# A hybrid layer on one core: the output projection's first half moved from behind the conv units to in front of them

## The chip, the cores and the metric

The kernel runs on one core of a Trainium2 chip. The metric is the device time of one execution in microseconds (us), as the median of several runs. The engines are TensorE (PE, the matmuls), VectorE (DVE), ScalarE (ACT), GpSimd (POOL) and SyncE (SP, which issues most DMAs). Each of them works through its own queue of instructions in order.

## What is computed

One layer over 576 frames (512 of a prompt, 64 of a running stream), 2048 wide, in float32:

```python
hn = rmsnorm(x, g_norm1)
q, k, v, gb, gc, hc = split(hn @ w_in)              # 3 x 1024 columns of heads, 3 x 1024 of conv
o_attn = stick_breaking_blocks(rmsnorm(q), rmsnorm(k), v)
u = gc * hc
o_conv = gb * causal_conv3(u)                       # 8 groups of 128 channels
mix = concat(rmsnorm(o_attn, g_attn_out), rmsnorm(o_conv, g_conv_out))
x = x + mix @ w_out                                 # first half of the rows: heads, second half: conv
h2 = rmsnorm(x, g_norm2)
x = x + (silu(h2 @ w_gate) * (h2 @ w_up)) @ w_down
```

Outputs are the new x, the new keys and values, and the last two rows of u. What matters here is `mix @ w_out`: its first half of the sum (over the 1024 head channels) needs only the attention, and its second half needs all conv groups.

## The kernel before

**Numbers in two parts.** Every float32 operand of a matmul is a pair of a rounded value and the rest (`split`, L222: a cast on ACT, a subtraction on DVE or POOL). A product of two operands takes three matmuls: high by high, low by high, high by low. Frames are cut in halves of 288 columns (`HALVES`).

**Seven products.** Where a weight block and the frames are each cut in 2 x 2 blocks, Winograd's form of Strassen's method does the work of eight block products in seven, with sums of blocks on either side. For the conv columns the sums of frames (`xs_dram`, made in `x_sums`, L581) are written to DRAM during the heads and loaded again (`load_sum`, L858, and L1111). For the first half of the output projection the sums of the normed head outputs are called forms; `head_forms` (L528) makes 28 blocks of them (7 forms, 4 blocks deep) from `o_half`, the two tiles that hold the attention's result.

**The stages.** (1) Heads: 24 column blocks of `w_in` by plain products, attention of one head beside the projection of the next. (2) Two conv groups by plain products (`conv_group`, L903, `STD` = 2, six column blocks). Beside them `head_forms` runs, spread over PE's work by a small planner: `Pipeline` (L66) counts a tick for each step of three matmuls, and a generator says with `yield n` after how many ticks its next instructions are placed. Each form is split into a staging tile and written to `form_dram`, 28 writes on SP (L553). (3) Nine conv units by seven products (`CU`, L934), six groups in pairs of u, u, b. (4) Eight output units by seven products over the forms, which are loaded back from `form_dram` in seven DMAs (`load_forms`, L1068). (5) The second half of the projection by plain products (`out_proj`, L1151) over the mix tiles of the conv groups, loaded from `mix_dram`. (6) The feed-forward part.

**Units and their order.** `conv_run(n, p)` does product p of unit n: 24 matmuls in a conv unit, 12 in an output unit. `conv_prepare(n, p)` (L967) casts and splits the weights of a product, four products ahead of PE (L1130), into four rotating places (`whl`); at product 6 it makes three sums of weight blocks on DVE (L974 to L976, the tile `s1`). `corder` (L1114) is the order of products, written out by hand. The raw weights lie in three places: two of 1 MB in `raw_tile`, and `raw_c` in the memory of the first attention tile; an output unit takes one of the first two for all its weights. `call_columns` (L942) loads the next weights when a place comes free. `done` (L1018) takes a finished block: a conv block goes through the taps, and `put_mix` (L515) scales it, adds its squares to the norm's sum and writes it to `mix_dram` on POOL's queue; an output block is added to the residual x in `x2`. The tiles of `put_mix`, and others, rotate in a ring of two (tag `hl`).

**Order on the engines.** PE works in the order of the text. For DVE, ACT and POOL, the compiler's list scheduler decides the order by what it reckons to be ready; SP's order is that of the text only in stretches with `manual_schedule` (before: from the last conv unit on, L1128). DMA loads are issued by SP and wait there, in order, for their place.

**At the seams.** Before the output units, the last conv unit has its products in another order (L1117), so that the places of the frame sums come free in time for the forms (L1132 to L1138). `open_out` (L1072) then opens the tiles for the residual and the mix, and `load_rest` and `group_scale` (L567) bring x and the norm's scale beside the output units.

Of the kernel before, what the change touches and what calls it, by code (L numbers as in the profile page):

```python
# [16 lines left out]
P = 128  # L17
# [77 lines left out]
def tile_hybrid_stream_step(  # L95
# [35 lines left out]
    form_dram = tc.dram_tile([FORMS, NH // 2, 2, P, HALF], F32, name="form_dram")  # L131
# [383 lines left out]
    def put_mix(g, i, src, gcol, acc, first):  # L515

        turns["mx"] = turns.get("mx", 0) + 1
        if "mx" in bt and turns["mx"] % 3 == 0:
            t = bt["mx"]
        else:  # L520
            t = tmp.tile([P, 2, HALF], F32R, tag="hl", name="mx")
        nc.scalar.activation(out=t[:, 0], in_=src, func=AF.Copy, scale=gcol)
        add_squares(acc, src, first)
        nc.vector.scalar_tensor_tensor(out=t[:, 1], in0=src, scalar=gcol, in1=t[:, 0].bitcast(F32),
                                       op0=ALU.mult, op1=ALU.subtract)
        nc.gpsimd.dma_start(out=mix_dram[i, g].rearrange("f p t -> p f t"), in_=t.bitcast(F32))

    def head_forms():  # L528
# [3 lines left out]
        turn = [0]  # L532
# [6 lines left out]
        yield 8  # L539
        for k in range(NH // 2):  # L540
            pair = o_half[k // 2][:, 2 * (k % 2) : 2 * (k % 2) + 2, :]
            four = pair.rearrange("p k (i t) -> p (k i) t", i=2)
            b11, b12, b21, b22 = (four[:, q, :] for q in range(4))
            for r in range(2):
                nc.vector.scalar_tensor_tensor(out=pair[:, r], in0=pair[:, r], scalar=col("ga", 2 * k + r), in1=acc_a,
                                               op0=ALU.mult, op1=ALU.mult)
            yield 2

            def put(f, src, lo_eng):
                t = bt["stage"][:, turn[0] % NP]  # L550
                turn[0] += 1
                split(t[:, 0], t[:, 1], src, lo_eng)
                nc.sync.dma_start(out=form_dram[f - 1, k].rearrange("f p t -> p f t"), in_=t.bitcast(F32))  # L553

            for f, src in ((1, b11), (2, b21), (3, b22)):
                put(f, src, nc.vector)
                yield 2
            for f, out, a, b in ((5, b11, b12, b11), (7, b12, b12, b22), (6, b22, b22, b11), (4, b21, b21, b22)):
                nc.gpsimd.tensor_tensor(out=out, in0=a, in1=b, op=ALU.subtract)
                yield 1  # L560
                put(f, out, nc.gpsimd if f in (5, 6) else nc.vector)
                yield 2
            if k == 1:
                bt["raw"] = apool.tile([P, 2048], F32, tag="oa", name="raw_c")
        load_sum(3)

    def group_scale(acc, dst, rows_of):  # L567

        four = cpool.tile([P, 2, 2, HALF], F32R, tag="uc", name="sqg")
        for i, (a, b) in enumerate(HALVES):  # L570
            sh, sl = four[:, i, 0], four[:, i, 1]
            split(sh, sl, acc[:, a:b])
            yield rows_of
            ss = channel_sums(sh, sl, a, b, "ssg")
            ms, t = (tmp.tile([P, HALF], F32, tag=tag, name=tag + "g") for tag in ("r", "sq"))
            rsqrt_mean(dst[:, a:b], ss, 8 * P, HALF, ms, t)
            yield rows_of
# [269 lines left out]
    def open_b():  # L847
# [14 lines left out]
    def open_units():  # L862
        cx = apool.tile([P, 1024 + UW + 2 * HALF], F32, tag="ob", name="cx")
        bt["mx"] = cx[:, 1024 + UW :].rearrange("p (f t) -> p f t", t=HALF).bitcast(F32R)
        bt["s1"] = cx[:, :1024].rearrange("p (j c) -> p j c", c=P)
        bt["c"] = cx[:, 1024 : 1024 + UW - 2]
# [27 lines left out]
    def put_o(g, i, t):  # L894
# [6 lines left out]
        put_mix(g, i, t, col("gc", g), bt["acc"][:, a:b], g == 0)  # L901

    def conv_group(g):  # L903
# [22 lines left out]
        if g == STD - 1:  # L926
            call_columns([2])
# [838 lines left out]
```

## Time and profile before

| | us |
|---|---|
| median of 3 runs | 2409.63 |
| lowest, highest | 2407.19, 2409.69 |
| the profiled execution | 2407.78 |
| its span, first to last instruction | 2406.1 |
| conv units, about | 504 to 711 |
| output units, about | 711 to 811 |
| second half of the projection, about | 811 to 912 |

Rows of the trace are read so. A row of the timeline has the start, the length, the engine, the line of the kernel, the operation, the tile written, an arrow and the tile read, the shape and a count; in brackets the idle time before it and what ended it. PEld is the loading of weights, which goes beside the matmuls. SPq rows are DMA issues: their length is that of the issue, not of the transfer. The clock that PE was granted is 0.997 of full speed over the whole span.

### The profile page before, as it was taken

To read this page: it belongs to the slowest core of one execution; us is meant where nothing else is said; L and a number is where in the kernel's file an instruction comes from. 1 tells how busy PE (TensorE), PEld (TensorE's weight loads), DVE (VectorE), ACT (ScalarE), POOL (GpSimd) and SP (SyncE) were. 2 spreads that over 40 slices of the span, in tenths; PEclk is the share of its full clock that TensorE was granted. 3 is DMA by queue.
4 is the path that set the end of the run, shared out by engine and by line. 5 is a ranking of instruction groups with operands and counts; after the bars stand their busy time and mean duration, and the time that the engine had idled before them with its cause. 6 is when DMAs were issued, how large, how long until landed. Compare 5 with 4: busy or idle time off the path is not lost.

```text
span 2406.1 us, 44221 instructions
## 1 busy us (share of the span) xinstructions
PE 2375.1 (99%) x17825; PEld 2363.2 (98%) x17825; DVE 1911.9 (79%) x2862; ACT 1166.1 (48%) x2091; POOL 293.9 (12%) x400
## 2 busy tenths in 40 slices
PE   8999999999999999999999999999999999999999
PEld 8999999999999999999999999999999999999999
DVE  7767776688888868988888888888888777887875
ACT  6656655444444445444444444444444444444454
POOL 1111111231112220000000000000000001431211
PEclk9999999999999999999999999999999999999999
DMA  7354433584367433444444434534444945885642
GB/s 255 116 152 139 143 111 95 188 277 125 101 213 253 143 129 107 148 145 150 135 135 150 152 118 155 160 112 157 150 128 142 335 139 188 231 234 196 201 130 80
DMA packets 504086, 386.05 MB, mean 160 GB/s; under 512 B 11855, under 2 KB 493001, under 8 KB 503881
## 3 DMA queue, kind: packets, MB, share of 16 engines
q1 hardware_dynamic: 496712, 371.40, 48.3%
q0 software_dynamic: 6448, 11.51, 2.1%
q8 instruction: 139, 2.28, 0.4%
q14 instruction: 67, 0.54, 0.1%
q10 hardware_dynamic: 720, 0.33, 0.0%
HBM read 296.47 MB, written 86.72 MB: 159 GB/s over the span
## 4 chain that ended last, share of the span: by engine, by line
PE 84%; DVE 8%; DMA 4%; ACT 2%; issue 1%; POOL 0%; SPq 0%; ACTq 0%; DVEq 0%; POOLq 0%
PE psy L1516 33%; PE psw L1516 16%; PE pj L214 12%; PE psx L1516 8%; PE pjo L214 4%; DVE whl L224 3%; PE psy L1006 2%; PE pw L1359 2%; DMA raw_a<-in_w_in_dram 1%; PE psw L1006 1%; PE psx L1006 1%; DMA raw_c<-in_w_in_dram 1%; DMA forms<-form_dram 1%; PE z L683 1%; ACT whl L223 0%
## 5 line engine op out<-in xcount | busy, mean ns | idle before, releaser
L224 DVE TENSOR_TENSOR whl<-raw_a,whl 128x1024 fp32r<-128x1024 f32 (+4 forms) x372 | 391.6, 1053 | 76.0 <-ACT whl L223 74.8
L1516 PE MATMUL psy<-t,whl 128*128 128x288 f32 x2916 | 436.6, 295 | 0.0
L1516 PE MATMUL psy<-h_s,whl 128*128 128x288 f32 x2724 | 410.9, 295 | 1.8 <-ACT part L1526 1.8
L223 ACT CAST whl<-raw_a 128x1024 fp32r<-128x1024 f32 (+4 forms) x372 | 327.0, 881 | 159.2 <-issue 37.1
L1516 PEld LDWEIGHTS psy<-t,whl 128*128 128x128 f32 x2916 | 402.8, 188 | 0.2
L214 PE MATMUL pj<-x,whi 128*128 128x288 f32 x1856 | 398.8, 300 | 0.3 <-DVE x L357 0.3
L1516 PEld LDWEIGHTS psy<-h_s,whl 128*128 128x128 f32 x2724 | 377.4, 188 | 2.3 <-ACT part L1526 2.2
L1516 PE MATMUL psw<-t,whl 128*128 128x288 f32 x2592 | 376.8, 295 | 0.0
L1516 PEld LDWEIGHTS psw<-t,whl 128*128 128x128 f32 x2592 | 353.7, 188 | 0.2
L214 PEld LDWEIGHTS pj<-x,whi 128*128 128x128 f32 x1856 | 307.7, 190 | 1.0 <-DVE x L357 0.6
L214 PE MATMUL pj<-x,wlo 128*128 128x288 f32 x928 | 275.2, 297 | 0.1
L224 DVE TENSOR_TENSOR whl<-raw_b,whl 128x1024 fp32r<-128x1024 f32 (+5 forms) x186 | 194.1, 1044 | 69.3 <-ACT whl L223 68.2
L223 ACT CAST whl<-raw_b 128x1024 fp32r<-128x1024 f32 (+5 forms) x186 | 161.1, 868 | 162.8 <-issue 69.4
L1526 ACT COPY part<-psy 128x288 f32<-128x288 f32 x237 | 94.4, 399 | 270.5 <-PE psy L1516 270.3
L214 PEld LDWEIGHTS pj<-x,wlo 128*128 128x128 f32 x928 | 175.8, 189 | 0.7 <-DVE wlo L424 0.3
L1516 PE MATMUL psx<-h_s,whl 128*128 128x288 f32 x1122 | 164.5, 294 | 0.0
L1516 PEld LDWEIGHTS psx<-h_s,whl 128*128 128x128 f32 x1122 | 154.0, 188 | 0.0
L1279 POOL DMA_DIRECT2D hid_dram<-form x3 | 2.2, 725 | 975.9 <-DVE form L224 974.0
L223 ACT CAST whl<-s 128x1024 fp32r<-128x1024 f32 (+5 forms) x79 | 70.1, 888 | 99.2 <-PE psw L1516 97.7
L177 DVE TENSOR_TENSOR wlo<-raw_a,whi 128x1024 fp32r<-128x1024 f32 (+1 forms) x80 | 98.2, 1242 | 7.7 <-ACT whi L176 6.1
L214 PE MATMUL pjo<-mixc,whi 128*128 128x288 f32 x512 | 101.7, 294 | 0.0
L176 ACT CAST whi<-raw_a 128x1024 fp32r<-128x1024 f32 (+1 forms) x85 | 85.6, 1024 | 18.4 <-PE pjo L214 8.6
(449 smaller groups left out, 3988.2 us busy)
## 6 DMA issues: line engine op xcount, KB each, us to landing
hid_dram<-form SPq DMA_DIRECT2D x147, 288.0 KB, 2.3
raw_a<-in_w_in_dram SPq DMA_DIRECT2D x41, 1024.0 KB, 6.4
raw_a<-in_w_gate_dram SPq DMA_DIRECT2D x23, 1024.0 KB, 6.2
raw_a<-in_w_up_dram SPq DMA_DIRECT2D x23, 1024.0 KB, 5.5
raw_b<-in_w_gate_dram SPq DMA_DIRECT2D x21, 1024.0 KB, 6.7
raw_b<-in_w_up_dram SPq DMA_DIRECT2D x21, 1024.0 KB, 6.6
h_s<-hid_dram SPq DMA_DIRECT2D x10, 2016.0 KB, 8.0
raw_a<-in_w_out_dram SPq DMA_DIRECT2D x16, 1024.0 KB, 5.2
```

The lines of the kernel that those rows point to most:

```text
L176: nc.scalar.copy(out=hi[:, a:b], in_=raw[:, a:b])
L177: lo_eng.tensor_tensor(out=lo[:, a:b], in0=raw[:, a:b], in1=hi[:, a:b].bitcast(F32), op=ALU.subtract)
L214: mm(ps, w_[:, k, csl], x_, start=(k == 0 and n == 0), stop=(k == nk - 1 and n == 2))
L223: nc.scalar.copy(out=hi, in_=src)
L224: (lo_eng or nc.vector).tensor_tensor(out=lo, in0=src, in1=hi.bitcast(F32), op=ALU.subtract)
L683: mm(zb[i], a_[:, kk], b_[:, q0:TP], start=(n == 0), stop=False, skip_group_check=True)
L1006: mm(ps, whl[:, w_, j, :], x_, start=(start and j == 0 and q == 0), stop=(j == m - 1 and q == 2), skip_group_check=True)
L1279: q.dma_start(out=hid_dram[fp][2 * n - 2 : 2 * n].rearrange("f p t -> p f t"), in_=t.bitcast(F32))
L1359: mm(pss[j, i], w_[:, k, j * P : (j + 1) * P], x_, start=(kk == 0 and k == 0 and n == 0), stop=(kk == 1 and k == 7 and n == 2))
L1516: mm(ps, whl[:, w_, j, :], x_, start=(start and j == 0 and q == 0), stop=(j == len(xs_) - 1 and q == 2), skip_group_check=True)
L1526: nc.scalar.copy(out=t, in_=st["y"])
```

## The change

The output units now come before the conv units, directly behind the two plain conv groups.

- **Forms stay on chip.** `head_forms` splits forms 1, 2, 3, 5, 6, 7 straight into three tiles (`ft`), which take the places that the frame sums had, and form 4 into the first attention tile's memory once its blocks have been used (two of its blocks are first made in a tile of the `hl` ring). Forms 1 and 2 are made for all four depths first, then 3, 5, 7, 6, and 4 last. `form_dram` goes, with 28 writes and 7 reads.
- **Residual.** Each output unit adds to two rows of x, loaded into one of two places in the second attention tile's memory (`load_residual`), and is stored to `oh_dram` (`store_half`); all of it is loaded into `x2t` at the end.
- **Frame sums.** The three big loads of frame sums (`load_sum`) are issued in the last output unit, each when the forms in its place have been used.
- **Weights.** `raw_c` and the taps' and `s1`'s tile are opened behind the output units (`open_groups`); an output unit's `s1` comes from the `hl` ring.
- **Last conv unit.** Its products run as 1, 2, 6, 3, 5, 7, 4, with products 3, 7 and 4 in banks of their own; the last groups' mix goes straight to its tile, the rest of the mix is loaded in seven pieces from `open_out` on, and the norm's scale is worked out half by half (`group_scale(1)`, `group_scale(0)`), with its column sums nine ticks behind their split. `out_proj` takes the second half of the frames first.
- **SP** keeps the order of the text from the end of the plain conv groups to the end of the units.

```diff
-    form_dram = tc.dram_tile([FORMS, NH // 2, 2, P, HALF], F32, name="form_dram")
+    oh_dram = tc.dram_tile([KD, P, T], F32, name="oh_dram")
...
     def head_forms():
...
+        def put(f, k, src, lo_eng):
+            split(ft[f][:, k, 0], ft[f][:, k, 1], src, lo_eng)
+
+        for r in range(2):
+            for k in range(NH // 2):
+                pair = o_half[k // 2][:, 2 * (k % 2) : 2 * (k % 2) + 2, :]
                 nc.vector.scalar_tensor_tensor(out=pair[:, r], in0=pair[:, r], scalar=col("ga", 2 * k + r), in1=acc_a,
                                                op0=ALU.mult, op1=ALU.mult)
+                yield 1
+                put(1 + r, k, blocks[k][2 * r], nc.vector)
                 yield 2
+        for k, (b11, b12, b21, b22) in enumerate(blocks):
+            put(3, k, b22, nc.vector)
+            yield 1
+            for f, out, a, b in ((5, b11, b12, b11), (7, b12, b12, b22), (6, b22, b22, b11)):
                 nc.gpsimd.tensor_tensor(out=out, in0=a, in1=b, op=ALU.subtract)
                 yield 1
+                put(f, k, out, nc.gpsimd if f in (5, 6) else nc.vector)
                 yield 2
+        moved = tmp.tile([P, 2, HALF], F32, tag="hl", name="t4")
...
+        ft[4] = apool.tile([P, NH // 2, 2, HALF], F32R, tag="oa", name="form4")
...
+    def group_scale(i):
+
+        a, b = HALVES[i]
+        sh, sl = parts("sqg")
+        split(sh, sl, bt["acc"][:, a:b])
+        yield 9
+        ss = channel_sums(sh, sl, a, b, "ssg")
...
-        bt["stage"] = bpool.tile([P, NP, 2, HALF], F32R, tag="t3", name="hf")
-        for q in (1, 2):
-            load_sum(q)
+        for q, (f, e) in {1: (1, 2), 2: (6, 7), 3: (5, 3)}.items():
+            t = bpool.tile([P, NP, 2, HALF], F32R, tag=f"t{q}", name=f"forms{q}")
+            ft[f], ft[e] = t[:, : NH // 2], t[:, NH // 2 :]
...
     def open_units():
+        ob = apool.tile([P, 2304], F32, tag="ob", name="ob")
+        bt["x2"] = [ob[:, q * 2 * T : (q + 1) * 2 * T].rearrange("p (k t) -> p k t", k=2) for q in range(2)]
+        bt["ob"] = ob
+        bt["s1"] = ob[:, :1024].rearrange("p (j c) -> p j c", c=P)
+        bt["c"] = ob[:, 1024 : 1024 + UW - 2]
+
+    def open_groups():
+        bt["mx"] = bt["ob"][:, 1024 + UW : 1024 + UW + 2 * HALF].rearrange("p (f t) -> p f t", t=HALF).bitcast(F32R)
+        bt["raw"] = apool.tile([P, 2048], F32, tag="oa", name="raw_c")
+        call_columns([2])
...
-    CU = [x for g in range(STD, NG, 2) for x in (("u", g), ("u", g + 1), ("b", g))]
-    NCU = len(CU)
-    CU += [("o", d) for d in range(DC)]
+    CU = [("o", d) for d in range(DC)]
+    NO = len(CU)
+    CU += [x for g in range(STD, NG, 2) for x in (("u", g), ("u", g + 1), ("b", g))]
+    LAST = len(CU) - 1
...
+            if n < NO:
+                s1 = tmp.tile([P, 2, HALF], F32, tag="hl", name="s1").rearrange("p f t -> p (f t)")
+                s1 = st["s1"] = s1[:, : m * P].rearrange("p (j c) -> p j c", c=P)
+            else:
+                s1 = st["s1"] = bt["s1"]
...
+            if (n, p_) in ((LAST - 1, 4), (LAST, 3)):
+                load_weight()
+            elif n >= NO or (n, 4 - p_) not in cregion:
                 call_columns([q])
...
+    def load_residual(n):
+        nc.sync.dma_start(out=bt["x2"][n % 2], in_=xt_dram[2 * n : 2 * n + 2].rearrange("k p t -> p k t"))
+
+    def store_half(n):
+        nc.sync.dma_start(out=oh_dram[2 * n : 2 * n + 2].rearrange("k p t -> p k t"), in_=bt["x2"][n % 2])
...
+        for i in (1, 0):
+            end = NG - 1 - i
+            for k in range(0, end, 2):
+                e = min(k + 2, end)
+                nc.sync.dma_start(out=mc[:, i, k:e].bitcast(F32), in_=mix_dram[i, k:e].rearrange("k f p t -> p k f t"))
+        for j in range(NP):
+            nc.sync.dma_start(out=x2t[j], in_=oh_dram[2 * j : 2 * j + 2].rearrange("k p t -> p k t"))
...
+    sp_mode = ExitStack()
+    sp_mode.enter_context(tc.manual_schedule(engines={mybir.EngineType.SP}))
...
     open_units()
+    for n in range(2):
+        load_residual(n)
+    corder = [(0, p_) for p_ in (1, 2, 6, 7, 5)]
+    for n in range(1, LAST + 1):
+        corder += [(n, 1), (n - 1, 3), (n - 1, 4), (n, 2), (n, 6)]
+        corder += [(n, p_) for p_ in ((7, 5) if n < LAST else (3, 5, 7, 4))]
+    for p_ in (6, 7):
+        conv_prepare(0, p_)
     for k_, (n, p_) in enumerate(corder):
         conv_run(n, p_)
         if k_ + 4 < len(corder):
             conv_prepare(*corder[k_ + 4])
+        if p_ == 2 and 1 <= n <= NO:
+            store_half(n - 1)
+        if p_ == 7 and 1 <= n < NO - 1:
+            load_residual(n + 1)
+        if n == NO - 1 and p_ in (2, 7, 3):
+            load_sum({2: 1, 7: 2, 3: 3}[p_])
+        if (n, p_) == (NO - 1, 4):
+            open_groups()
...
-                for i, (a, b) in enumerate(HALVES):
+                for i, (a, b) in reversed(list(enumerate(HALVES))):
```

More of the change, by code (lines that the diff above doesn't have):

```diff
@@ L539, in head_forms @@
         yield 8
+        blocks = []
         for k in range(NH // 2):
@@ new lines, in head_forms @@
+        for k, (b11, b12, b21, b22) in enumerate(blocks):
+            if k < 2:
+                nc.gpsimd.tensor_tensor(out=moved[:, k], in0=b21, in1=b22, op=ALU.subtract)
+                blocks[k][2] = moved[:, k]
+            else:
+                nc.gpsimd.tensor_tensor(out=b21, in0=b21, in1=b22, op=ALU.subtract)
+            yield 1
+        ft[4] = apool.tile([P, NH // 2, 2, HALF], F32R, tag="oa", name="form4")
+        for k in range(NH // 2):
+            put(4, k, blocks[k][2], nc.vector)
+            yield 1
@@ L1049, in conv_run @@
             st["u2"] = kept("t")
+        elif n == LAST:
+            if p_ == 3:
+                st["c"] = misc("ps3")[:, :HALF]
+                conv_multiply(st["c"], n, 3, True)
+            elif p_ == 5:
+                conv_multiply(st["y"], n, 5, False)
+                open_out()
+                st["part"] = kept("acc")
+                done(0, 1, st["c"], st["part"])
+            elif p_ == 7:
+                w = ps_z.tile([P, 512], F32, tag=f"z{n % 2 + 1}", name="psw")[:, :HALF]
+                conv_multiply(w, n, 7, True)
+                done(1, 1, w, st["part"])
+                st["w"] = tmp.tile([P, HALF], F32, tag="ms", name="part", bufs=1)
+                nc.vector.tensor_tensor(out=st["w"], in0=w, in1=st["u2"], op=ALU.add)
+                pipe.spawn(group_scale(1))
+            else:
+                w = ps_z.tile([P, 512], F32, tag="z0", name="ps4")[:, :HALF]
+                conv_multiply(w, n, 4, True)
+                done(1, 0, w, st["w"])
+                rest = group_scale(0)
+                pipe.spawn(rest, next(rest))
         elif p_ == 7:
```

114 lines of the change are left out of this document (25 added, 89 removed).

## The prediction, on record before the run

> **What bounds the kernel now.** I read the page's engine totals first, then TensorE's waits between 440 and 960 us (where every step of the change lies), then the windows of that stretch.
>
> ```profile
> span 2406.1 us, 44221 instructions
> PE 2375.1 (99%) x17825; PEld 2363.2 (98%) x17825; DVE 1911.9 (79%) x2862; ACT 1166.1 (48%) x2091; POOL 293.9 (12%) x400
> ```
>
> TensorE (PE) is busy for 99% of the span. The change removes and adds no matmul (counts below), so it can only win the places where PE stands still, or make new ones. Where they are (us in total, times, longest):
>
> ```profile
> PE psy L1006 <- DMA forms<-form_dram: 6.1, 1, 6.1
> PE psy L1006 <- DVE whl L224: 4.0, 1, 4.0
> ```
>
> Two waits stand out. What follows each costs too (start, length, count, idle before):
>
> ```profile
> 701.61 3.17 PE psx L1006 x24
> 731.37 1.59 PE psw L1006 x12
> ...
> 514.44 4.78 PE L1006 MATMUL psy<-x,whl 128*128 128x288 f32 x23 [4.04 <-DVE whl L224]
> 723.99 7.38 PE L1006 MATMUL psy<-forms,whl 128*128 128x288 f32 x36 [6.10 <-DMA forms<-form_dram]
> ```
>
> A product takes 3.17 us with 24 matmuls and 1.59 us with 12, so 0.132 us a matmul. After the wait of 4.04 us 23 matmuls took 4.78 us instead of 3.04 (1.7 lost again); after 6.10 us 36 took 7.38 instead of 4.76 (2.6). The sum is best read from how many matmuls each 20 us window lacks (windows: us, PE busy and count, PEld, DVE, ACT, POOL, PE clock, DMA share, GB/s; the first row is a full one):
>
> ```profile
> 540.00:560.00 20.00, 20.00 (x153) 20.00 (x152) 17.97 (x23) 8.15 (x11) 1.23 (x7) 1.00 0.36 106
> ...
> 500.00:520.00 20.00, 15.96 (x110) 15.72 (x109) 19.19 (x22) 8.26 (x15) 9.17 (x13) 0.91 0.90 300
> 520.00:540.00 20.00, 19.51 (x148) 19.28 (x147) 12.70 (x16) 7.40 (x9) 0.87 (x1) 1.00 0.75 247
> ...
> 680.00:700.00 20.00, 19.83 (x148) 19.36 (x147) 16.42 (x22) 7.86 (x10) 0.85 (x2) 1.00 0.52 166
> 700.00:720.00 20.00, 17.89 (x133) 17.39 (x132) 18.27 (x34) 9.61 (x22) 6.21 (x8) 1.00 1.05 367
> 720.00:740.00 20.00, 16.01 (x103) 16.04 (x104) 10.98 (x17) 5.89 (x12) 4.01 (x5) 0.83 0.73 271
> ...
> 800.00:820.00 20.00, 19.21 (x146) 18.97 (x145) 16.85 (x27) 9.94 (x18) 4.08 (x4) 1.00 0.52 163
> ```
>
> They lack 43+5+5+20+50+7 = 130 matmuls of 0.131 us: **17.0 us**, all of it at the seams of the stage. That is the most the change can win. In the middle (540 to 680 us in conv units, 740 to 800 us in output units) nothing is lost.
>
> **The change, part by part.**
>
> *Unchanged:* 8 output units of 7 products with 12 matmuls (672) and 9 conv units of 7 with 24 (1512), only in the other order. DVE gains two additions of 288 columns in the last unit (0.46 us each by the L1029 row below).
>
> *Removed, 17.0 us.* The seam at 503.76 us goes: PE waited there for weights that landed late in the third place (`raw_c`). So does the seam at 710 to 731 us: 28 form writes and 7 form reads vanish, and no output unit follows a conv unit any more. With it goes the turned-round last conv unit (680 to 720 us), and the seam at 800 us. What is late next, at each new seam:
>
> *Seam 1, head stage to output units.* Unit 0 needs forms 1 and 2 at once, forms 6, 7, 5 from its third product on, and three weight sums. Its products start where the first conv unit's did, and the forms are the same instructions:
>
> ```profile
> 503.76 3.33 PE L1006 MATMUL psy<-x,whl 128*128 128x288 f32 x24
> ...
> 505.43 1.05 DVE L224 TENSOR_TENSOR hf<-o_ob,hf 128x288 fp32r<-128x288 f32 x1 [0.18 <-ACT hf L223]
> ...
> 494.76 1.38 DVE L224 TENSOR_TENSOR whl<-raw_a,whl 128x1024 fp32r<-128x1024 f32 x1 [0.34 <-ACT whl L223]
> 497.77 1.23 DVE L224 TENSOR_TENSOR whl<-raw_a,whl 128x1024 fp32r<-128x1024 f32 x1 [0.49 <-ACT whl L223]
> ...
> 715.61 0.61 ACT L223 CAST whl<-raw_a 128x512 fp32r<-128x512 f32 x1
> 715.90 0.68 DVE L974 TENSOR_TENSOR cx<-raw_a 128x512 f32<-128x512 f32 x1
> 716.50 0.68 DVE L224 TENSOR_TENSOR whl<-raw_a,whl 128x512 fp32r<-128x512 f32 x1
> ```
>
> Before, the last form was done at 506.5. The two weight splits at 494.8 and 497.8 shrink from 2.61 to 1.36 us, so DVE is clear at 505.3. The three sums take 3 x 0.68, the cast 0.61, the lower part 0.68: product 6 is ready at 508.6. PE arrives at 503.8 + 2 x 1.59 = 506.9. **I take 1.7 us**, short enough to keep the clock. Form 4 comes last but is needed last: PE reaches it after seven products, at 514.9. Below, the bound is 0 (DVE may take the sums before the last forms); above, 16 + 2.6 us, if the sums wait for their buffer (last rival). The residual of unit 0 is new in front of DVE's first addition, and what DVE has behind that waits as well:
>
> ```profile
> o_ob<-xt_dram SPq DMA_DIRECT2D x8, 576.0 KB, 4.7
> ```
>
> Its place is free at 506.5, so it lands at 511.2; behind it DVE has the split for the sixth product, done at 512.3, and PE gets there at 508.6 + 3 x 1.59 = 513.4. Covered by 1.1 us; without cover it costs what it is late.
>
> *Output units.* Each has 7 x 1.59 = 11.1 us. Its weights are asked for when a place comes free, and the next unit's residual is queued on SP behind them:
>
> ```profile
> 759.93 4.76 PE psy L1006 x36
> ...
> 762.34 0.38 SPq L955 DMA_DIRECT2D raw_a<-in_w_out_dram  x1
> raw_a<-in_w_out_dram SPq DMA_DIRECT2D x15, 1024.0 KB, 5.2
> ...
> 760.00:780.00 20.00, 20.00 (x153) 20.00 (x152) 18.17 (x29) 9.53 (x18) 4.51 (x5) 1.00 0.77 262
> ```
>
> The weights are issued 2.4 us after product 7, land 5.2 later, and 576 KB more take 1.5 (at the rate below): the residual is there 9.1 us after product 7, the addition that needs it is due at 5 x 1.59 = 7.9. DVE stands for 1.2 us a unit. Operands are split four products ahead, 4.8 us less 1.3 for cast and split, so 3.5 us of cover: **0**. DVE is busy 18.17 of 20 us, though; 1.2 of 11.1 us more fills it, and 0 to 4 us stay in the range. The finished half's store:
>
> ```profile
> x_dram<-x SPq DMA_DIRECT2D x3, 576.0 KB, 2.8
> ```
>
> It stands on SP behind POOL's last addition, and its buffer is refilled two products (3.2 us) later: 0.4 us to spare.
>
> *Seam 2, output to conv units.* Three loads of 2304 KB, formerly issued at 458 and 514 us, now wait until the forms in their places have been used.
>
> ```profile
> 465.00:470.00 5.00, 5.00 (x40) 5.00 (x39) 4.52 (x10) 4.30 (x8) 0.30 (x1) 1.00 1.08 391
> L860 SPq DMA_DIRECT2D xs_t<-xs_dram x3: 359/366/2342, 457.8 to 514.0; - x3
> ...
> xs_t<-xs_dram SPq DMA_DIRECT2D x3, 2304.0 KB, 9.9
> ...
> 685.44 1.23 DVE L974 TENSOR_TENSOR cx<-raw_c 128x1024 f32<-128x1024 f32 x1 [2.20 <-DMA raw_c<-in_w_in_dram]
> 689.22 1.05 ACT L223 CAST whl<-raw_a 128x1024 fp32r<-128x1024 f32 x1 [0.17 <-DVE raw_a L976]
> ```
>
> Count from the end of product 2 of output unit 7. SP then queues a half store (0.59 MB), the first load (2.36 MB), at 5.6 us conv unit 8's second weights (1.05), the second load, at 9.8 the third, at 11.4 unit 9's first weights. Data flow from 1.7 us at 0.39 MB a us: unit 8's second weights are there after 4.0 MB, at 12.1, and seen at about 12.5. Then three sums (1.23 each), cast 1.05, lower part 1.23: 18.6. PE wants it five output and two conv products later: 5 x 1.59 + 2 x 3.17 = 14.3. Wait 4.3, and 1.7 for the clock as after 4.04: **6.0**. The last weights land at 27.5, are split at 30; PE needs them at 30. Ends: 0 (the weights overtake the first load) and 9 (those too are late by 3).
>
> A rule speaks against this seam: the Trainium skill, "DMA: Bandwidth & Descriptors", section "Bandwidth", puts what one core gets from HBM at about 358 GB/s. By it 9.8 MB would take 2 us longer than at 391, seam 2 cost some 8 us, and the forecast be 2 us later. The window at 465 us shows 391 GB/s for these very loads, so the trace disagrees.
>
> *Seam 3, conv units to the second half.* The norm's two column sums now stand 9 ticks (0.4 us each) behind their splits. The chain from a last product, in an earlier unit:
>
> ```profile
> 702.08 0.46 DVE L1029 TENSOR_TENSOR cv<-psw,part 128x288 f32<-128x288 f32 x1 [0.18 <-ACT part L1015]
> ...
> 705.75 1.11 POOL L511 TENSOR_TENSOR acc_c<-acc_c,sqm 128x288 f32<-128x288 f32 x1 [11.51 <-ACT sqm L510]
> ...
> 715.27 0.43 ACT L223 CAST sqg<-acc_c 128x288 fp32r<-128x288 f32 x1
> 715.53 0.45 DVE L224 TENSOR_TENSOR sqg<-acc_c,sqg 128x288 fp32r<-128x288 f32 x1
> ```
>
> From 702.08 to 706.86 is 4.8, with cast and split 5.7, and 0.2 to start: 5.9. The first sum stands 3.17 + 0.8 = 4.0 behind its product: wait 1.9; the second then finds its data. The mix loads, 13 groups of 0.29 MB from the end of product 5 on, feed the half that starts 6.3 us later: the first pair is there at about 4.5, the third at 7.5 for a use at 8. **2.0 us**; ends 0 and 6 (both sums wait in full, and the loads).
>
> *Sum:* 1.7 + 0 + 6.0 + 2.0 = 9.7 us new for 17.0 old: 7.3 less. The profiled execution took 2407.78 us (span 2406.1), 1.9 under the runs' median of 2409.63 and inside their 2407.19 to 2409.69. So 2400.5 by the one, 2402.3 by the other; **I say 2401.5**, with 2396 to 2405 for this case.
>
> **Rivals.** *All covered:* sums go early, waits stay under a product's lead; 3 us at seam 2 only, 14 less: 2395. For it: DVE's order on the chip follows readiness, not the text, and the short waits have little in front of them. Against: 9.8 MB have to come through.
>
> *Nothing won:* seam 2 costs 9, a full DVE in the output units 3, seams 1 and 3 as above: 15.7 for 17.0, hence 2407.4. For it: 91% DVE; against: 1.2 us of lateness is within the lead.
>
> *Slower:* the sums' buffer. Unit 0's sum tile comes from the `hl` ring of two, held by form 4's moved blocks and by the last group's mix tiles, which are free only when their write has landed:
>
> ```profile
> 508.96 0.73 POOL L526 DMA_DIRECT2D mix_dram<-mx  x1 [1.82 <-DVE mx L524]
> ...
> DMA to landing us min/median/max: 2.6/5.4/10.8
> ```
>
> With that write issued at 509.0 and landing 5.4 to 10.8 us later the sums begin at 514.4 to 519.8, product 6 is ready 3.3 later, and PE waits 10.9 to 16.3 and loses 2.6 to the clock: 13.5 to 18.9 at seam 1. Middle 16.2: 24.2 in all, 7 slower, **2416**. It decides from 9.0 us at seam 1, a landing after 510. For it: these rows. Against: the write can be issued once DVE is clear at 505.3, and form 4's buffer may be free first.
>
> The Trainium skill, "TensorE: Matmul & The Clock Gate", Part 1, lets the clock fall only after an idle window of about 3.4 us. The trace agrees in the one row of 4.04 us, which lost 1.7 more. By it, a seam shorter than that pays only its wait, as seams 1 and 3 are counted above.
>
> **Numbers.** Forecast 0.34, all covered 0.12, nothing won 0.27, slower 0.27. A measurement tells about 0.2% (4.8 us) from no change, so faster is the first two less a hundredth for the forecast's edge, 0.45, same 0.28, slower 0.27. Range 2394 to 2415.
>
> **What would show it.** Right: no form wait; output units at 11.1 us; PE's longest wait at product 6 of the first conv unit, for its split, behind the second weights. Wrong: a wait over 4 us at product 6 of output unit 0 (seam 1), PE idle inside the output units (DVE), or sums at the end that wait over 3 us.

## The result: slower, by 0.57%

The changed kernel took 2422.55 us (median of 4 runs, 2422.03 to 2425.97), the kernel before 2409.66 (4 runs, 2407.19 to 2411.96) on the same chip: ratio 1.0057, 95% interval 1.0039 to 1.0074. That is 12.9 us slower where 7.3 less were forecast. The profile of the changed kernel is of its slowest execution, the 2425.97 us one, and its span is 18.2 us longer than that of before. Some 2 us of this lie in the first 100 us, ahead of everything the change touches (PE busy 90.0 of 100 us there, 92.1 before), and 1.6 in the feed-forward part (360 matmuls from 967 to 1017 us, where before had 372 from 950 to 1000).

From the page of the changed kernel, its first line and the line of engine totals:

```profile
span 2424.3 us, 44116 instructions
PE 2377.7 (98%) x17825; PEld 2363.5 (97%) x17825; DVE 1914.0 (79%) x2864; ACT 1165.9 (48%) x2091; POOL 299.3 (12%) x397
```

The matmuls are the same 17825, so the time can only lie in the waits between them and in the clock at which they run. TensorE's waits between 440 and 960 us (us in total, times, longest), in place of the two of before:

```profile
PE psy L1036 <- ACT whl L223: 16.4, 2, 9.3
PE psy L1036 <- DVE whl L224: 2.9, 3, 1.7
PE ssg L471 <- ACT sqg L223: 2.4, 2, 1.8
PE psy L1036 <- ACT part L1045: 1.6, 4, 0.7
PE ssg L472 <- DVE sqg L224: 0.7, 1, 0.7
```

The form wait is gone, as forecast, and two waits for split weights have taken its place, 9.3 and 7.1 us. What each stretch lost is read as in the prediction, from the windows of the changed kernel (a full one holds 153 matmuls):

```profile
500.00:520.00 20.00, 10.43 (x76) 9.87 (x75) 12.39 (x24) 7.23 (x15) 8.62 (x14) 0.83 0.63 207
520.00:540.00 20.00, 20.00 (x139) 20.00 (x140) 17.16 (x26) 8.48 (x17) 5.05 (x5) 0.91 0.27 89
...
580.00:600.00 20.00, 18.85 (x140) 18.38 (x140) 17.87 (x26) 9.04 (x18) 6.89 (x6) 1.00 0.43 151
600.00:620.00 20.00, 16.80 (x125) 16.38 (x123) 10.53 (x16) 4.75 (x8) 4.79 (x4) 0.98 1.05 333
620.00:640.00 20.00, 14.38 (x94) 14.06 (x95) 12.67 (x14) 7.73 (x9) 0.00 (x0) 0.77 1.01 336
...
820.00:840.00 20.00, 17.38 (x128) 16.69 (x127) 16.18 (x34) 9.46 (x21) 2.77 (x3) 1.00 1.06 399
840.00:860.00 20.00, 19.50 (x148) 19.26 (x147) 15.91 (x26) 10.09 (x19) 6.06 (x6) 1.00 0.53 175
```

Seam 1 (first two rows) lacks 77 + 14 = 91 matmuls of 0.131 us; the output units between 540 and 600 us lack 20; seam 2 lacks 28 + 59 = 87; one window in the conv units lacks 8; seam 3 lacks 25 + 5 = 30. The table gives the same count for seven of the runs below, in matmuls and, for the changed kernel, in us. Each column is one execution, and those of one kernel differ by up to 7 us (e4: 2408.50 to 2415.64), so a difference of a few matmuls tells nothing:

| stretch | forecast us | changed us | changed | e1 | e4 | e6 | e5 | e11 | e12 |
|---|---|---|---|---|---|---|---|---|---|
| seam 1, 500 to 540 | 1.7 | 11.9 | 91 | 38 | 38 | 38 | 91 | 89 | 38 |
| output units, 540 to 600 | 0 | 2.6 | 20 | 20 | 16 | 18 | 29 | 16 | 21 |
| seam 2, 600 to 640 | 6.0 | 11.4 | 87 | 81 | 74 | 82 | 102 | 62 | 87 |
| conv units, 640 to 800 | 0 | 1.0 | 8 | 2 | 2 | 5 | 10 | 18 | 11 |
| seam 3, 800 to 860 | 2.0 | 3.9 | 30 | 34 | 22 | 32 | 33 | 38 | 23 |

The new losses sum to 236 matmuls, 30.9 us, for the 17.0 us of before: 13.9 more, where the medians differ by 12.9.

**Seam 1.** From the timeline of the changed kernel, engine by engine (start, length, what, idle before and releaser): PE, DVE, POOL, and the chain of work:

```profile
506.44 1.75 PE L1036 MATMUL psy<-forms,whl 128*128 128x288 f32 x12
508.02 1.74 PE L1036 MATMUL psx<-forms,whl 128*128 128x288 f32 x12
519.06 0.61 PE L1036 MATMUL psy<-forms,whl 128*128 128x288 f32 x1 [9.29 <-ACT whl L223]
519.95 3.01 PE L1036 MATMUL psy<-forms,whl 128*128 128x288 f32 x11 [0.28 <-DVE whl L224]
```

```profile
508.91 0.52 DVE L526 SCALAR_TENSOR_TENSOR mx<-gbr,vec,mx 128x288 fp32r<-128x288 f32 x1 [0.60 <-ACT mx L524]
515.59 0.69 DVE L1002 TENSOR_TENSOR s<-raw_a 128x512 f32<-128x512 f32 x1 [5.12 <-DMA mix_dram<-mx]
```

```profile
510.04 0.72 POOL L529 DMA_DIRECT2D mix_dram<-mx  x1
```

Read backwards: PE stands 9.3 us at product 6 of output unit 0 for its split weights; the first weight sum (L1002) starts only at 515.59, after DVE stood 5.12 us for the landing of a mix write; that write was issued at 510.04. This is the "slower" rival, row by row. Some 2 us of the 2.3 on top of the waits are clock: 12 matmuls took 0.61 + 3.01 us where 12 take 1.59, and the two windows show a granted clock of 0.83 and 0.91.

**Seam 2.** The chain of work of the changed kernel from unit 7's product 2 (first row) to product 6 of the first conv unit:

```profile
600.62 1.59 PE psx L1036 x12
...
608.63 0.61 DVE whl L224
...
609.26 9.16 DMA raw_a<-in_w_in_dram
...
620.13 1.13 DVE raw_a L1003
...
625.04 1.15 DVE whl L224
...
626.23 4.69 PE psy L1036 x23
```

The place of the second weights is freed by a split at 609.24, their load takes 9.16 us, and sums, cast and split take until 626.2. The two waits are 8.8 us of the 11.4; after them the clock was low again (0.77 in the second window).

**Output units and seam 3.** SP, DVE and PE of the changed kernel, one fence for each:

```profile
562.18 0.37 SPq L979 DMA_DIRECT2D raw_a<-in_w_out_dram  x1
...
573.91 0.37 SPq L979 DMA_DIRECT2D raw_a<-in_w_out_dram  x1
```

```profile
567.27 0.69 DVE L1002 TENSOR_TENSOR s<-raw_a 128x512 f32<-128x512 f32 x1 [1.60 <-DMA raw_a<-in_w_out_dram]
...
579.30 0.69 DVE L1002 TENSOR_TENSOR s<-raw_a 128x512 f32<-128x512 f32 x1 [1.91 <-DMA raw_a<-in_w_out_dram]
```

```profile
556.43 1.75 PE L1036 MATMUL psw<-forms,whl 128*128 128x288 f32 x12
...
582.10 5.02 PE L1036 MATMUL psy<-forms,whl 128*128 128x288 f32 x36 [0.66 <-ACT part L1045]
...
825.23 0.40 PE L471 MATMUL ssg<-sqg,oner 128*128 128x288 f32 x1 [1.85 <-ACT sqg L223]
829.71 0.40 PE L472 MATMUL ssg<-sqg,oner 128*128 128x288 f32 x1 [0.69 <-DVE sqg L224]
```

DVE stands for each unit's weights, and PE for a copy that comes after it; at the end both column sums wait. The first three rows make a round: weights issued at 562.18 are used from 567.27 on, 5.1 us later, and DVE works 6.6 us more until the split that ends at 573.9 frees the place for the next ones. That is 11.7 us where PE needs 11.1. In the kernel before, the same work of DVE, from its first sum to the next issue, took 5.2 us (768.24 to 773.43).

### The profile page after: what moved, and what is told of

Same layout as the page of the kernel before. It is cut to its first block, busy times and chain, and to the rows that moved or that the text cites. A ratio compares the mean times of both kernels' runs of the same rounds, so it can differ in the third digit from the quotient of the medians.

```text
span 2424.3 us, 44116 instructions
## 1 busy us (share of the span) xinstructions
PE 2377.7 (98%) x17825; PEld 2363.5 (97%) x17825; DVE 1914.0 (79%) x2864; ACT 1165.9 (48%) x2091; POOL 299.3 (12%) x397
## 4 chain that ended last, share of the span: by engine, by line
PE 79%; DVE 9%; DMA 5%; ACT 3%; issue 2%; POOL 1%; SPq 0%; ACTq 0%; DVEq 0%; POOLq 0%
PE psy L1559 33%; PE psw L1559 16%; PE pj L214 8%; PE psx L1559 8%; PE pjo L214 4%; PE psy L1036 3%; DVE whl L224 2%; PE pw L1402 2%; DMA raw_a<-in_w_in_dram 1%; PE psw L1036 1%; DMA raw_a<-in_w_out_dram 1%; DMA o_ob<-xt_dram 1%; DVE wlo L177 1%; PE psx L1036 1%; DMA xs_dram<-xs_out 0%
## 5 line engine op out<-in xcount | busy, mean ns | idle before, releaser
L223 ACT CAST whl<-s 128x1024 fp32r<-128x1024 f32 (+5 forms) x87 | 75.1, 863 | 105.7 <-PE psw L1559 97.5
```

The costliest lines, as they stand in the source:

```text
L223: nc.scalar.copy(out=hi, in_=src)
```

## The experiments

The theory after the result: seam 1 is the buffer ring (as in the "slower" rival), seam 2 is too many bytes ahead of the second weights. The rivals: at seam 1 DVE is late in any case; at seam 2 the chain behind the weights binds, not the bytes. Each run is given with its ratio to before, timed on the same chip.

### e1_sums_own_place: the sum tile out of the ring

```diff
-                s1 = tmp.tile([P, 2, HALF], F32, tag="hl", name="s1").rearrange("p f t -> p (f t)")
+                s1 = rpool.tile([P, T], F32, tag="R", name="s1", bufs=2)
```

> The changed kernel, but the sum tile s1 of the output units comes from the place of the attention's column scale (idle by then) and not from the hl ring of two. Theory (ring): DVE's stand of 5.1 us for the mix write goes, PE's wait of 9.3 us at product 6 of output unit 0 falls to under 3 us, and since one place only lets the next unit's sums start behind the last one's split, DVE no longer stands for the weights inside the units: 11.1 us a unit and no longer 11.4 to 12.0. In all 9 to 12 us less than 2422.6, so 2411 to 2414. Rival (DVE or the forms are late anyway): PE still waits 6 us or more at that product and the time is 2419 to 2423.

Measured 2412.58 us, ratio 1.0023 (1.0014 to 1.0033): 0.34% less than the changed kernel, about 8 us. Seam 1 fell from 91 to 38 matmuls. PE of this kernel, product 6 of unit 0:

```profile
508.90 3.04 PE L1036 MATMUL psy<-forms,whl 128*128 128x288 f32 x12 [3.01 <-ACT part L1045]
```

The wait for the split is gone; what is left, 3.0 us and 1.3 of clock, is a wait for ACT's copy of product 1 (product 6 is summed onto the same buffer). So the ring is shown as the cause of the 9.3 us. The second half of the theory, that the units go back to 11.1 us, did not come true: between 540 and 600 us they still lack 20.

### e2_weights_first: unit 8's second weights ahead of the loads of the frame sums

```diff
-        if n == NO - 1 and p_ in (2, 7, 3):
-            load_sum({2: 1, 7: 2, 3: 3}[p_])
+        if n == NO - 1 and p_ in (7, 5):
+            load_sum({7: 1, 5: 2}[p_])
         if (n, p_) == (NO - 1, 4):
             open_groups()
+            load_sum(3)
```

> The changed kernel, but the first load of frame sums is issued behind conv unit 8's second weights (after product 7 of output unit 7, where the second load stood), the second after product 5, and the third behind unit 9's first weights. Theory (order of the queue): the weights land about 5 us after their issue, not 9.2, PE's waits of 7.1 and 1.7 us at product 6 of unit 8 fall to about 4 in all, and seam 2 loses 4 to 7 us of its 11.4: 2416 to 2419. Rival (bandwidth: the same 9.8 MB have to come through before unit 9, in any order): the wait only moves to product 7 or to unit 9, the time is 2421 to 2424.

Measured 2423.48 us, ratio 1.0068 (1.0053 to 1.0083). PE of this kernel:

```profile
620.97 5.82 PE L1036 MATMUL psy<-xs_t,whl 128*128 128x288 f32 x24 [5.24 <-DMA xs_t<-xs_dram]
...
648.12 2.12 PE L1036 MATMUL psy<-xs_t,whl 128*128 128x288 f32 x14 [1.10 <-DVE whl L224]
```

The wait changed its name, as the rival had it. The weights are used 6.0 us behind their issue (608.01 to 614.02) instead of 9.3, but the first sum of frames is 5.2 us late, and the second conv unit's weights a little. Seam 2 lacks 64 matmuls in place of 87, the conv units 31 in place of 8: nothing is won.

### e3_scale_later and e4_all_three

e3 lets the norm's column sums come 14 ticks behind their splits instead of 9; e4 is e1, e2 and e3 together.

```diff
-        yield 9
+        yield 14
         ss = channel_sums(sh, sl, a, b, "ssg")
```

> The changed kernel, but the column sums of the norm's scale stand 14 ticks behind their split in place of 9 (2 us later on PE). Theory (sums placed too early): PE's waits of 1.85 and 0.69 us at the sums go, 2 to 3 us less: 2420 to 2421. Rival (the end of the stage is late as a whole, PE then waits for the scale or the mix): the same 2.5 us come back as waits in the second half of the projection, 2422 to 2424.

> The three edits before together. If the seams are independent, the gains add: 9 to 12, 4 to 7 and 2 to 3 us, so 2401 to 2408, under the 2409.7 of the kernel before. If a later seam takes back what an earlier one gives (the loads of seam 2 come earlier into the same queue), 2408 to 2414.

e3: 2421.14 us, ratio 1.0059 (1.0044 to 1.0074); the waits of the column sums fell from 1.85 and 0.69 us to 0.28, and seam 3 from 30 to 21 matmuls, about 1 us, which the total can't tell. e4: 2411.77 us, ratio 1.0024 (1.0014 to 1.0034), the same as e1 alone; the gains do not add, as the second of its two expectations says.

### e5_half_loads: the 7 MB start earlier

```diff
+        nc.sync.dma_start(out=t[:, a:b].bitcast(F32), in_=xs_dram[q, a:b].rearrange("j f p t -> p j f t"))
...
+    HL = {1: ((1, 0),), 2: ((1, 1),), 6: ((2, 0),), 7: ((2, 1),), 5: ((3, 0),), 3: ((3, 1),)}
```

> Only the loads of the frame sums change: six halves instead of three wholes, each into the place of a form of the output projection as soon as the product that read that form is done, so that the 7 MB start at about 596 us instead of 603.7 us. Theory (seam 2 is lost because 9 MB start too late): the first sum stands some 8 us earlier, the second weights of the first conv unit land by about 612 instead of 618.5, and the 11.4 us that lack at 600-660 us fall to 3-6 us: 5 to 8 us below the changed kernel, ratio to before 1.002-1.0035. Rival (the transfers of that stretch are bound by their bytes whatever their start, and earlier loads only delay the weights and residuals of the output units): 9-11 us still lack at seam 2, or the units lose as much as the seam gains; ratio 1.005 or more. Seam 1 keeps its wait of 9 us in both.

Measured 2426.38 us, ratio 1.0071 (1.0058 to 1.0084); seam 2 lacks 102. PE of this kernel:

```profile
623.24 0.61 PE L1038 MATMUL psy<-forms,whl 128*128 128x288 f32 x1 [7.71 <-ACT whl L223]
625.64 5.67 PE L1038 MATMUL psy<-forms,whl 128*128 128x288 f32 x23 [1.79 <-DVE whl L224]
```

SP of this kernel, the first half load and the second weights:

```profile
598.43 0.65 SPq L874 DMA_DIRECT2D forms<-xs_dram  x1
...
608.02 1.32 SPq L988 DMA_DIRECT2D raw_a<-in_w_in_dram  x1
```

The first load is issued 9.6 us ahead of the weights, where it was 5.5 in the changed kernel (603.74 and 609.26). Still PE waits longer, not less: three halves now stand ahead of the weights instead of one whole load. The theory of the late start falls, and the rival's 1.005 or more came true.

### e6_one_place: is the ring also what stretches the units?

```diff
+                if "so" not in bt:
+                    bt["so"] = rpool.tile([P, T], F32, tag="R", name="s1", bufs=2)[:, : 2 * HALF]
+                s1 = st["s1"] = bt["so"][:, : m * P].rearrange("p (j c) -> p j c", c=P)
```

> The sum tile of the output units stands in one place of its own, outside the ring of two. Theory (a ring of two lets the sums of the next unit go ahead of this unit's residual adds and splits, and DVE, in order, then stands for the weights): units back to 11.1 us each, the 2.5 us that lack between 540 and 600 us gone on top of seam 1's 8 us; about 11 us below the changed kernel, ratio 1.001. Rival (the units are stretched by something else, the residual loads or ACT): seam 1 as in the run with two places of its own (5 us lost), the units still lack 15 or more matmuls, ratio 1.0023 as there.

Measured 2414.99 us, ratio 1.0025 (1.0017 to 1.0034), as e1. The units still lack 18 between 540 and 600 us, so the rival holds: the ring does not stretch them.

### e7_combined and e8_combined_twice

```diff
-            tt(out=s1, in0=st["a21"], in1=st["a22"], op=ALU.add)
             tt(out=st["a21"], in0=st["a21"], in1=st["a11"], op=ALU.subtract)
-            tt(out=st["a11"], in0=s1, in1=st["a11"], op=ALU.subtract)
+            tt(out=s1, in0=st["a21"], in1=st["a22"], op=ALU.add)
+            tt(out=st["a11"], in0=s1, in1=st["a11"], op=ALU.add)
+            st["s1"], st["a11"] = st["a11"], s1
...
+                conv_multiply(st["y"], n, 1, True)
+                coper[0, 1] = whl
+                conv_multiply(st["x"], n, 1, True)
```

(The last three lines are e8's alone.) In both, the weights of product 5 of the last conv unit stand in a place that the output weights are loaded into before they are split, so that product's values are not the reference's; its size and number are.

> One place for the sum tile, the loads in halves, the scale's wait five products later, and the three sums of a unit in an order in which the sum of product 7 is made first, those of product 6 second (one sum less ahead of product 6's split). If the seams' losses add: seam 1 some 4 us, units 0-1, seam 2 3-5, seam 3 2-3 against 17.0 us before: 2 to 6 us below before, ratio 0.9975-0.999. If seam 2 is bound by bytes, 9-11 us there and ratio 1.001-1.003.

> As the combined kernel, and product 1 of output unit 0 is computed twice (12 matmuls more, 1.6 us), once for the sum of products 1 and 6 and once under product 2, so that product 6 need not wait for ACT's copy of product 1 behind the evictions of the last head group. Theory (the 3.0 us wait at product 6 is that copy's place in ACT's order): the wait goes, or falls to the weights' split; 1 to 2 us below the combined kernel. Rival (the split of product 6 is late by as much anyway): the wait stays with another name and the time is 0 to 1.6 us above the combined kernel.

e7: 2420.3 us, ratio 1.0049 (1.0036 to 1.0061), with the half loads of e5 in it and a wait of 7.66 us for the weights at seam 2. That is above both of its expectations: seam 2 lacks 99 matmuls, the units from 540 to 600 us 30, seam 3 49. e8: 2418.85 us, ratio 1.0041 (1.0027 to 1.0055). PE of e8 at seam 1, product 6:

```profile
509.19 0.40 PE L1040 MATMUL psy<-forms,whl 128*128 128x288 f32 x1 [0.65 <-ACT whl L223]
510.12 1.74 PE L1040 MATMUL psy<-forms,whl 128*128 128x288 f32 x11 [0.53 <-DVE whl L224]
```

In e7 PE waited 3.06 us here for the copy. Without it the wait becomes 1.2 us for the split, at full clock; the 12 matmuls more cost 1.6. So the copy was what ended last there, and DVE's split is close behind it. The 1.4 us between the totals of e7 and e8 are less than their scatter.

### e11_no_frame_loads: the 7 MB taken away

The kernel with half loads, and with none of them issued, so that the conv units read the forms that stand there and their values are not the reference's:

```diff
+    HL = {}
```

> The three loads of frame sums (7 MB) are left out; the conv units read the old forms that stand in their places, so the second half's values are not the reference's, with the same number of products, splits and other transfers. Sum tile and seam 1 as in the changed kernel. Theory (the second weights of the first conv unit are late because they share the transfers' rate with 7 MB): they land 4 to 6 us behind their issue instead of 9.2, PE's two waits at seam 2 shrink from 8.8 us to 1-4, and the time falls 5 to 8 us below the changed kernel, ratio 1.002-1.0035. Rival (what binds is the chain behind the region's release: weights, three sums, cast, split, and DVE's and ACT's order): the waits stay at 6 us or more, ratio above 1.004.

Measured 2416.82 us, ratio 1.0034 (1.0021 to 1.0047). The issue of the second weights, DVE's first sum on them, and PE, in this kernel:

```profile
606.27 0.37 SPq L988 DMA_DIRECT2D raw_a<-in_w_in_dram  x1
...
612.17 1.23 DVE L1004 TENSOR_TENSOR ob<-raw_a 128x1024 f32<-128x1024 f32 x1 [4.18 <-DMA raw_a<-in_w_in_dram]
...
617.53 0.61 PE L1038 MATMUL psy<-forms,whl 128*128 128x288 f32 x1 [3.73 <-ACT whl L223]
619.68 5.20 PE L1038 MATMUL psy<-forms,whl 128*128 128x288 f32 x23 [1.54 <-DVE whl L224]
```

The weights are used 5.9 us behind their issue instead of 9.3, as the theory of the bytes had it; the waits fall from 8.8 to 5.3 us, between the two expectations. Seam 2 still lacks 62 matmuls, 8.1 us, with none of the bytes. So by these profiles the bytes cost 3.3 of its 11.4 us; the other 8.1 go to the place of the weights being freed late, their own load, the three sums, cast and split behind it, and the clock. The ratio fell by more, by 0.0023 or some 5.5 us, which is in the theory's range; the execution profiled here is the slowest of its five (2420.00 us), and the intervals are too wide to tell 3.3 from 5.5.

### e10_seven_whole and e9_seven_first: a shorter chain in every unit

```diff
-        corder += [(n, 1), (n - 1, 3), (n - 1, 4), (n, 2), (n, 6)]
-        corder += [(n, p_) for p_ in ((7, 5) if n < LAST else (3, 5, 7, 4))]
+        corder += [(n, 1), (n - 1, 3), (n - 1, 4), (n, 2)]
+        corder += [(n, p_) for p_ in ((7, 6, 5) if n < LAST else (6, 3, 5, 7, 4))]
```

Product 7 needs one sum, product 6 two of them; e9 also loads product 7's frames in halves, and early. Both have e6's one place for the sum tile and e3's later scale in them, so they are to be held against e6's 1.0025.

> One place for the output units' sum tile, the scale's wait five products later, and in every unit but the last product 7 ahead of product 6, with the sums in the order that serves this (product 7 needs one, product 6 two of the three); the load of the sum that product 7 reads goes first. If ACT's copy of product 1 was what product 6 waited 3 us for at seam 1, half of that wait is covered by product 7 (1.6 us); if the chain of three sums behind the second weights binds seam 2, 2.4 us go there; if the bytes bind, the wait there becomes one for the sums' load. Chain theory: 3-5 us below the kernel with all three edits, ratio 1.0000-1.0012. Bytes theory: 1-2 us below it, ratio 1.0015-1.002.

> As the kernel with product 7 first, and the load of product 7's sum in two halves, each into the place of a form as soon as that form is read, so that 1.2 MB start about 8 us earlier and the second weights of the first conv unit find less ahead of them; the other two sums stand behind those weights. If the bytes bind seam 2: 2-4 us below the kernel with whole loads, ratio 0.9990-1.0005. If the chain behind the weights binds: within 1 us of it.

e10: 2421.61 us, ratio 1.0064 (1.0052 to 1.0077); e9: 2420.63 us, ratio 1.0057 (1.0044 to 1.0069). PE of e10, two output units in a row and then seam 2:

```profile
550.13 5.07 PE L1043 MATMUL psy<-forms,whl 128*128 128x288 f32 x36 [0.54 <-ACT part L1052]
562.09 5.07 PE L1043 MATMUL psy<-forms,whl 128*128 128x288 f32 x36 [0.54 <-ACT part L1052]
...
610.33 0.40 PE L1043 MATMUL psw<-xs_t,whl 128*128 128x288 f32 x1 [0.97 <-ACT whl L223]
611.66 3.33 PE L1043 MATMUL psw<-xs_t,whl 128*128 128x288 f32 x23 [0.94 <-DVE whl L224]
```

At seam 2 the first wait did shrink, from 8.8 to 1.9 us. But both expectations missed the price: a unit now takes 11.96 us instead of 11.1, since product 5 follows product 6 on the same buffer and stands 0.54 us for ACT's copy every time, in the conv units as well (41 matmuls lack there); the other 0.3 us go with the end and the restart of PE's matmuls around that wait. In the old order product 7 between them hid that copy. e9 came out 1 us from e10, as its expectation has it if the chain binds.

### e12_both_shortened: the short chain at seam 2 alone

e4's edits, the order and sums of e9 only in the first conv unit, and the next unit's weights ahead of the last half load:

```diff
+        corder += [(n, p_) for p_ in ((7, 6, 5) if n == NO else (6, 7, 5) if n < LAST else (6, 3, 5, 7, 4))]
...
             open_groups()
+            load_sum(3, 1)
...
+    HL = {1: ((2, 0),), 2: ((2, 1),), 7: ((1, 0), (1, 1)), 5: ((3, 0),)}
```

> The kernel with all three edits (sum tiles in places of their own, loads behind the weights, scale later), and at seam 2 alone both causes shortened: the first conv unit runs product 7 ahead of 6 with one sum ahead of product 7's split instead of three, the load of the sum that product 7 reads goes in two halves into the places of forms already read, ahead of the second weights, the two other sums behind them, and the next unit's weights stand ahead of the last half load. All other units keep product 6 ahead of 7, so the 0.5 us wait for a copy in every unit should not come. If the losses of seam 2 are the bytes ahead of the weights and the chain of sums behind them: its 9.7 us fall to 4-6, 2406-2408.5 us where before stands at 2407.3, ratio 0.9990-1.0008. Rival (the stretch moves its bytes no sooner, and the wait only passes on to the weights of the second conv unit): seam 2 at 8 us or more, ratio 1.0015-1.0025.

Measured 2414.55 us, ratio 1.0034 (1.0021 to 1.0048). PE of this kernel at seam 2:

```profile
606.59 0.61 PE L1044 MATMUL psw<-forms,whl 128*128 128x288 f32 x1 [2.59 <-ACT whl L223]
607.92 5.70 PE L1044 MATMUL psw<-forms,whl 128*128 128x288 f32 x23 [0.72 <-DVE whl L224]
...
617.33 3.44 PE L1044 MATMUL psy<-x,whl 128*128 128x288 f32 x24 [0.54 <-ACT part L1053]
622.20 0.40 PE L1044 MATMUL psy<-x,whl 128*128 128x288 f32 x1 [1.43 <-ACT whl L223]
623.46 8.00 PE L1044 MATMUL psy<-x,whl 128*128 128x288 f32 x47 [0.86 <-DVE whl L224]
```

The rival's mechanism holds, at a ratio even above its 1.0025: the first wait is 3.3 us, but the clock loses 2.4 again (23 matmuls in 5.70 us instead of 3.3), and the time comes back as a wait for the copy and one for the second conv unit's weights, again with clock behind it: 87 matmuls, as in the changed kernel. No version tried beats the kernel before; e1, e4 and e6 are the nearest, at 1.0023 to 1.0025.

## Why the prediction was wrong, point by point

The forecast was 7.3 us less and the windows show 13.9 more, a miss of 21.2 us. It splits into seam 1 (10.2), seam 2 (5.4), output units (2.6), seam 3 (1.9) and the conv units (1.0). Of the signs named beforehand for being wrong, the first was met: a wait over 4 us at product 6 of output unit 0.

- **Removed, 17.0 us: right.** No form wait and none of the old seams is left.
- **Seam 1, 1.7 us: the step that failed.** "DVE is clear at 505.3 ... product 6 is ready at 508.6" left out the wait for the sums' buffer, which stood beside it as the "slower" rival, given 0.27. Its argument against itself ("the write can be issued once DVE is clear at 505.3, and form 4's buffer may be free first") held only in small part: the write has to wait for the last plain group's gates (DVE's row at 508.91). Counted from the first product of the units (503.76 before, 506.44 now) it was issued at 3.6 us where before it was 5.2. From the issue it landed 5.5 us later, near the median of the row quoted; the seam cost 11.9 us, below the rival's 13.5 to 18.9 by about those 1.6 us, with the same mechanism. The rival decided "from 9.0 us at seam 1", and it did. Taking the ring away gave 8 us back (e1). Even then 1.7 was too little: 5.0 us stayed, 3.0 of them the copy of product 1, which the forecast did not have on its list (e8).
- **Output units, 0:** the windows show 2.6 us. DVE's wait for weights, put at 1.2 us a unit and covered, was 1.6 to 1.9 us, because the place of the next weights was freed later: they were issued 4.2 us behind the end of product 7 (556.43 + 1.59), not 2.4. Own places for the sums did not cure this (e1, e6). By the rows above the load and DVE's work up to the release make a round of 11.7 us, longer than PE's 11.1; why DVE takes 6.6 us for its part, and not the 5.2 of before, was not taken apart by a run and stays open.
- **Seam 2, 6.0 us: mechanism right, size off.** PE's wait was at product 6 of the first conv unit, for its split behind the second weights, as forecast. Counted from the end of unit 7's product 2 (602.2), the weights were issued at 7.1 instead of 5.6, there at 16.2 instead of 12.5, and split at 24.0 instead of 18.6, in part because two conv evictions stood between the sums on DVE; PE came at 14.4, as forecast (14.3). So the wait grew from 4.3 to 8.8 us, and the clock took 2.6 where 1.7 were forecast. The bytes, from which the forecast worked out when the weights land, are worth some 3.3 us (e11).
- **The rate at seam 2:** the windows from 600 to 640 us show 333 and 336 GB/s, not the 391 that I took. In steps of 4 us it is 335 to 360 while the second weights are on their way (608 to 620), and 391 right behind them (620 to 628). With the 358 of the Trainium skill, "DMA: Bandwidth & Descriptors", section "Bandwidth", the prediction had 8 us for this seam, which was nearer, though for a reason that carries less than half of the loss. That section gives the 358 as the share of a core whose neighbour streams too, and here one core runs, so the 391 of the trace does not speak against it.
- **Seam 3, 2.0 us:** the first column sum waited 1.85 us (forecast 1.9). The second did not find its data (0.69), and the last weight split 0.5 more; 3.9 in the count, of which the later scale gave back about 1 (e3).
- **Chances and range:** 2422.55 lies above the range's 2415. The "slower" case held the mechanism, but its 2416, which the range left outside, took seam 1 at 16.2 us, 4.3 too much, and the other seams at their forecast sizes.

## What to carry to other kernels

Before new work takes a buffer from a ring, find who holds the ring's places and what frees them: here a write's landing, whose issue and delay both stood in the trace of before, decided 8 us. A seam between two pipelined stages is a chain (place freed, load, sums, split), and shortening one link hands the wait to the next one, so price the whole chain, with the other evictions that stand between its links on the same engine. An order of products that looks free may be what hides a copy: swapping two of them cost 0.85 us in every output unit.

## What the hardware showed that was not expected

A wait of less than 3.4 us can also slow TensorE's clock, but not each one does. After 3.01 us of idling (e1, above) 12 matmuls took 3.04 us instead of the 1.75 of a full group, and after 2.59 and 0.72 us (e12) 23 took 5.70 instead of 3.3. Shorter waits did it too; these are the same three products of an output unit, twice in e8 and once in e7:

```profile
549.77 6.56 PE L1040 MATMUL psy<-forms,whl 128*128 128x288 f32 x36 [1.88 <-ACT part L1049]
...
586.68 6.55 PE L1040 MATMUL psy<-forms,whl 128*128 128x288 f32 x36 [1.74 <-ACT part L1049]
```

```profile
554.39 5.07 PE L1040 MATMUL psy<-forms,whl 128*128 128x288 f32 x36 [1.55 <-ACT part L1049]
```

In e8 the granted clock was 0.66 from 550 to 555 us, and 1.5 us were lost on top of the wait; in e7 nothing was. After 0.97 and 0.94 us (e10) 23 matmuls took 3.33, nothing lost, but after 1.05 and 0.56 us (e8, at 805 us) 23 took 4.86. The prediction named the Trainium skill, "TensorE: Matmul & The Clock Gate", Part 1, for an idle window of about 3.4 us. In these runs waits from 1.6 us on, in one piece or in two, lost clock in some places, and others of up to 1.9 us kept it. So a seam shorter than 3.4 us does not pay only its wait, and the measurement decides; what tells the two kinds apart no run here shows. The remainder of seam 1 and the shortened seam 2 thus paid for the clock too, which is part of why shortening their waits won so little.
